# Opening of a two-block transformer kernel: all keys accumulated by groups of two k-tiles as the modulation arrives, with the output gates' projections between the keys' convolutions

## The chip, the core and the metric

The kernel runs on one core of a Trainium2 chip. The metric is the device time of one execution in microseconds. The engines are TensorE (PE, its weight loads PEld), VectorE (DVE), ScalarE (ACT), GpSimd (POOL) and SyncE (SP), which issues the transfers.

## What is computed

A token sequence x (256 tokens, 1024 features) goes through a first block that also reads a context ctx (256 tokens), and then through two layers of feed-forward, mixer, feed-forward. The change lies at the start of the first block. Cut to that:

```
shift, scale, gate       = split(silu(c) @ w_mod + b_mod, 3)
shift_c, scale_c, gate_c = split(silu(c_ctx) @ w_mod + b_mod, 3)
h  = rmsnorm(x, norm_w) * (1 + scale) + shift
hc = rmsnorm(ctx, norm_w) * (1 + scale_c) + shift_c
qkv, beta, decay, kb, vb = split(h @ w_state)      # the same for hc, all but q
za, qb, zb, ga, gb       = split(h @ w_rest)
q, k, v = split(silu(short_conv(qkv)))             # 5 taps, 4 heads of 128
oa = gated_delta_rule(q, k, v, g(decay), sigmoid(beta))   # chunks of 64, both directions
ob = attention(rope(norm(qb)), rope(norm(kb)), vb)
y  = sigmoid(ga) * (ya @ w_proj_a) + sigmoid(gb) * (yb @ w_proj_b)
x  = x + gate * (y @ w_out)
```

All data are f32. The projections run as three products in fp32r: each operand is split into a rounded part and its remainder, and low x high, high x high and high x low are added.

## The kernel before

Activations lie transposed: feature on the partition, 8 k-tiles of 128 features, 256 tokens (T) on the free axis. A weight panel is 128 x 1024 f32 (512 KB). `wload` (L93) brings it into one of seven `raw` buffers through SP's queue, ScalarE rounds it into `wh` (L98), VectorE makes the remainder `wl` (L99), of each of which there are four. `mm3` (L102) runs the 24 products of one output tile of 128 features by 256 tokens, L110 to L112.

The order of each engine's instructions is not written out: a planner works it out when the program is built, from the order of the trace, from priorities (`high_priority(offset)` puts a block ahead by that many places; `prior`, L773, does it for a generator) and from its own estimates of durations. `tc.issue_after(ins)` adds an order only: instructions of the block that run on the engine of `ins` are issued behind it. Each engine then runs its list in order. PSUM has eight banks: `pj` 2, `ms` 2, `ch` 3, `md` 1.

**The opening, `b1_hidden` (L921).** The shift and scale of x and ctx (columns of `w_mod`, 2 x 1024) are made in four groups g of 256 features, which are two k-tiles. `mods(g)` (L947) loads the weights of a group. The shift of groups 0 and 2 is made on VectorE: a panel is multiplied by a row of silu(c) or silu(c_ctx), spread over all partitions by `mod_row` (L726), and summed (L954), eight such instructions. The other six products of 256 columns run on TensorE with two stationary columns (c and c_ctx, tile `cc`) and the raw weights as the moving operand, 8 products each (`psm`, L967), one PSUM tile of two rows; ScalarE copies the rows out (L969) and TensorE transposes them to columns (`m1t`, L972). `stats` (L939) squares and adds the 8 k-tiles of x or ctx, sums them over the partitions (`pss`, L165), takes the power on GpSimd (L170), spreads it (`rb`, L173) and multiplies the tiles (L945). `hidden` (L980) applies scale and shift on ScalarE (L984) and splits into `hH` and `hL`. Order of the trace: mods(0), x, mods(1), ctx, stats of x, stats of ctx, mods(2), hidden(0) of x, mods(3), the rest of hidden. All of `b1_hidden` is traced ahead of the first projection.

**Then, `block1` (L782):** the row for c_2, constants, `b1_bd` (L1038: beta and decay, `w_bd`, 48 products with 16 stationary columns), `gates` (L1119: decays, their sums, the factors E0 and E1 through `gps` and four `gdf` products, all banks from `ch`), `b1_keys` (L1076: for each of four heads `b1_both` (L1029) runs 24 products for x and 24 for ctx into `psk`; five-tap convolution on VectorE, L1009; four transposes `ktp` into a `ch` bank, L1095; squares on ScalarE), the first step of `gdn_inverse` (L1257, products of the keys with each other, times E), the kv projection of the attention (`att_k`, `att_v`), and the values of four heads with a step of the inverse between each. After that follow 32 projections of x alone, `rest` (L817): the output gates gb (8, tanh into `tb`), qb (4), q (4), zb, za, ga, each with steps of the inverse, the attention and the chain of the delta rule (`gdn_chain`) between. The block ends with the merge: `branch("w_b")`, `gdn_out` (L1449, gives `ya`), `branch("w_a")`, and `w_out`.

The heart of the opening's TensorE part:

```
for i, raw in enumerate(raws):                       # L964
    for j in range(4):
        k = 4 * i + j
        nc.tensor.matmul(o, c2[:, k, :], raw[:, j * T : (j + 1) * T], start=k == 0, stop=k == 7)
```

Of the kernel before, what the change touches and what calls it, by code (L numbers as in the profile page):

```python
# [37 lines left out]
class Kern:  # L38
# [63 lines left out]
    def mm3(self, ps, W, h, kw, kh, first, last):  # L102
# [4 lines left out]
        for i, (a, b) in enumerate(zip(kw, kh)):  # L107
# [4 lines left out]
            mm(ps, H[:, s], hL[:, b, :T], start=False, stop=l)  # L112
# [669 lines left out]
    def block1(self):  # L782
        nc, A = self.nc, self.A
        with ExitStack() as c:
# [5 lines left out]
            gates = self.gates()  # L790
            gb = self.b1_bd(hx, hc)
            for _ in self.prior(gates(gb), 600):
                pass
            self.b1_rope_consts()
            self.b1_keys(hx, hc)
            inv = self.prior(self.gdn_inverse(), 1500)
            next(inv)
            ak = self.att_k(self.b1_both(A["w_kv"][0], hx, hc))
            next(ak)
            self.att_v(self.b1_both(A["w_kv"][1], hx, hc))  # L800
            for h in range(4):
                next(inv)
                self.b1_value(h, hx, hc)
            four = lambda n, t: self.yy.tile([P, KD, T + 2], F32, tag=t, name=n)
            pair = lambda n, t: four(n, t)[:, :, :T].rearrange("p (i h) t -> p i h t", i=2)
            Q2 = pair("Q2", "hHc")
            self.qT, self.qr = Q2[:, 0], Q2[:, 1]

            self.MT = four("MT", "hLc").rearrange("p k t -> p (k t)")[:, : 4 * 512].rearrange("p (b n m t) -> p b n m t", b=2, n=2, t=P)
            self.Db = pb.tile([P, 2, 4, P], F32, tag="Ec", name="Db")  # L810
            nc.gpsimd.memset(self.MT, 0.0)
            nc.gpsimd.memset(self.Db, 0.0)
            self.nqa = pb.tile([P, 2, 2, 4], F32, name="anq")
            self.nqg = pb.tile([P, 2, 4], F32, name="gnq")
# [21 lines left out]
            for kind, n in (("gb", 8), ("qb", 4), ("q", 4)):  # L836
                for i in range(n):
                    if kind == "gb" and i == 4:
                        next(ak)
# [81 lines left out]
    def b1_hidden(self):  # L921
# [24 lines left out]

        def mods(g, after=None):  # L947
            a = slice(2 * g, 2 * g + 2)
            fast = g % 2 == 0
            if fast:  # L950
                for k in (2 * g, 2 * g + 1):
                    raw = self.wraw(self.A["wmod_sh"][g + k % 2], 1024)
# [788 lines left out]
```

## Time and profile before

| | us |
|---|---|
| median of 3 runs | 1442.99 |
| lowest, highest run | 1441.73, 1444.32 |
| profiled execution | 1442.31 |
| its span | 1440.5 |
| TensorE busy in it | 1403.3 (97%) |
| VectorE busy | 1141.0 (79%) |
| ScalarE busy | 771.0 (54%) |
| GpSimd busy | 85.7 (6%) |
| mean rate of the transfers | 211 GB/s |

The span is that of one profiled execution; its instructions are laid out by engine, with the idle time before each and what ended it. The execution took 1.8 us more than the span, and 0.7 us less than the median. A product of plain f32 operands leaves two records in the trace, one of fp32r operands or a transpose leaves one. Lengths of products overlap, as they are pipelined: the time from start to start counts.

### The profile page before, as it was taken

The numbers are of one execution on the slowest core, as the hardware profiler recorded it, in microseconds if no ns is written. First come the engines' busy times: TensorE is split into PE (matmuls) and PEld (weight loads), VectorE is DVE, ScalarE is ACT, GpSimd is POOL, SyncE is SP. The second block draws the span as 40 slices with busy tenths as digits, with TensorE's granted clock in tenths as the row PEclk, the third lists the DMA queues.
The fourth block names the chain that finished last, engine by engine and source line by source line (L and its number), as shares of the span: only waits on it lengthen the run. The fifth ranks groups of instructions, "written<-read, shape, count | busy, mean of one in ns | idle before, by whom it ended". The sixth has DMA issues, their size and how long they took to land. (4 is left out here: it accounts for less than half of the span.)

```text
span 1440.5 us, 27393 instructions
## 1 busy us (share of the span) xinstructions
PE 1403.3 (97%) x10786; PEld 1305.3 (91%) x10786; DVE 1141.0 (79%) x2124; ACT 771.0 (54%) x1315; POOL 85.7 (6%) x87
## 2 busy tenths in 40 slices
PE   7999989999999999999999999999999999999998
PEld 4798867889999989998899998999989998899997
DVE  6769888858887887888897797977688889796554
ACT  4654586644644446447564444544446357554442
POOL 0011100012100001001100001000011010100000
PEclk9999999999999999999999999999999999999999
DMA  8524545635688985557568897688774557577562
GB/s 317 195 64 124 150 147 174 222 103 164 198 288 276 323 286 182 176 153 252 171 202 303 271 356 243 201 283 286 237 255 158 172 175 234 175 242 241 172 199 70
DMA packets 94833, 303.98 MB, mean 211 GB/s; under 512 B 18128, under 2 KB 20432, under 8 KB 94448
## 3 DMA queue, kind: packets, MB, share of 16 engines
q1 hardware_dynamic: 89824, 299.90, 63.3%
q8 instruction: 85, 1.39, 0.4%
q10 hardware_dynamic: 4432, 1.11, 0.4%
q0 software_dynamic: 448, 1.21, 0.3%
q14 instruction: 44, 0.36, 0.1%
HBM read 300.09 MB, written 2.10 MB: 210 GB/s over the span
## 5 line engine op out<-in xcount | busy, mean ns | idle before, releaser
L98 ACT CAST wh<-raw 128x1024 fp32r<-128x1024 f32 (+3 forms) x407 | 414.6, 1021 | 288.2 <-PE psd L121 89.1
L99 DVE TENSOR_TENSOR wl<-raw,wh 128x1024 fp32r<-128x1024 f32 (+3 forms) x407 | 481.5, 1187 | 94.5 <-ACT wh L98 93.6
L111 PE MATMUL psf<-hH,wh 128*128 128x256 f32 x1088 | 306.1, 281 | 0.0
L112 PE MATMUL psf<-hL,wh 128*128 128x256 f32 x1088 | 305.6, 281 | 0.0
L110 PE MATMUL psf<-hH,wl 128*128 128x256 f32 x1088 | 305.4, 281 | 0.0
L121 PE MATMUL psd<-gHL,wh 128*128 128x512 f32 x704 | 244.3, 392 | 0.0
L744 DVE CUSTOM_DVE_ANT_0 raw<-raw,mrow 128x1024 f32<-128x1024 f32 x152 | 184.5, 1219 | 69.7 <-DMA raw<-in_wmod 68.1
L110 PEld LDWEIGHTS psf<-hH,wl 128*128 128x128 f32 x1088 | 205.6, 189 | 0.0
L112 PEld LDWEIGHTS psf<-hL,wh 128*128 128x128 f32 x1088 | 205.5, 189 | 0.0
L111 PEld LDWEIGHTS psf<-hH,wh 128*128 128x128 f32 x1088 | 204.8, 188 | 0.0
L122 PE MATMUL psd<-gHL,wl 128*128 128x256 f32 x704 | 196.8, 280 | 0.0
L121 PEld LDWEIGHTS psd<-gHL,wh 128*128 128x128 f32 x704 | 132.2, 188 | 29.0
L110 PE MATMUL psp<-hH,wl 128*128 128x256 f32 x512 | 149.6, 292 | 2.4 <-DVE wl L99 2.4
L111 PE MATMUL psp<-hH,wh 128*128 128x256 f32 x512 | 148.2, 289 | 0.0
L112 PE MATMUL psp<-hL,wh 128*128 128x256 f32 x512 | 147.0, 287 | 0.0
L122 PEld LDWEIGHTS psd<-gHL,wl 128*128 128x128 f32 x704 | 132.2, 188 | 0.0
L110 PEld LDWEIGHTS psp<-hH,wl 128*128 128x128 f32 x512 | 97.7, 191 | 5.5 <-PE psp L112 1.7
L112 PEld LDWEIGHTS psp<-hL,wh 128*128 128x128 f32 x512 | 97.7, 191 | 1.6 <-issue 1.0
L111 PEld LDWEIGHTS psp<-hH,wh 128*128 128x128 f32 x512 | 97.3, 190 | 1.2 <-issue 0.7
L249 ACT ACTIVATE ft<-psf 128x256 f32<-128x256 f32 x68 | 26.2, 386 | 112.2 <-PE psf L112 112.2
L157 POOL TENSOR_TENSOR sqa<-sqa,sq 128x256 f32<-128x256 f32 x36 | 31.3, 868 | 593.9 <-issue 481.3
L252 ACT CAST gHL<-ft 128x256 fp32r<-128x256 f32 x88 | 35.7, 406 | 28.1 <-DVE ft L250 22.3
(513 smaller groups left out, 2789.3 us busy)
## 6 DMA issues: line engine op xcount, KB each, us to landing
raw<-in_ffn_gu SPq DMA_DIRECT2D x176, 512.0 KB, 4.4
raw<-in_wmod SPq DMA_DIRECT2D x144, 512.0 KB, 4.5
raw<-in_ffn_dn SPq DMA_DIRECT2D x64, 448.0 KB, 4.1
raw<-in_win SPq DMA_DIRECT2D x56, 512.0 KB, 4.3
raw<-in_w_rest SPq DMA_DIRECT2D x32, 512.0 KB, 3.8
raw<-in_ffn_dn SPq DMA_DIRECT2D x32, 512.0 KB, 4.6
raw<-in_wmod_sc SPq DMA_DIRECT2D x12, 512.0 KB, 7.4
raw<-in_wout_a SPq DMA_DIRECT2D x16, 384.0 KB, 4.0
```

The costliest lines, as they stand in the source:

```text
L98: nc.scalar.copy(H[:, :n], raw[:, :n])
L99: nc.vector.tensor_sub(L[:, :n], raw[:, :n], H[:, :n].bitcast(F32))
L110: mm(ps, L[:, s], hH[:, b, :T], start=f, stop=False)
L111: mm(ps, H[:, s], hH[:, b, :T], start=False, stop=False)
L112: mm(ps, H[:, s], hL[:, b, :T], start=False, stop=l)
L121: mm(ps, H[:, s], h[:, b, :, :T], start=first and i == 0, stop=False)
L122: mm(ps[:, 1, :], L[:, s], h[:, b, 0, :T], start=False, stop=last and i == len(kw) - 1)
L157: self.seng.tensor_add(self.sqa, self.sqa, o)
L249: nc.scalar.activation(t, ps[:, 0, :], AF.Silu)
L252: nc.scalar.copy(gH[:, f, :], t)
L744: nc.vector.tensor_tensor_reduce(raw, raw, row, op0=ALU.mult, op1=ALU.add, scale=1.0, scalar=0.0, accum_out=t[:, j : j + 1])
```

## The change

Layout on the host: `w_mod`'s shift and scale columns lie by group (`wmod_s`: for each g, shift then scale, two raws each), and the keys' weights by group too (`w_kg[g]`: k-tiles 2g and 2g+1 of all four heads in one panel).

`b1_hidden` loads x and ctx ahead of the modulation's weights, and `w_bd` next. All sixteen modulation raws go to TensorE. The stationary operand has 32 columns (c, c_ctx and thirty zeros); of the four k-tiles in a raw each writes another 32 partitions of one bank, so four partial sums stand below one another. ScalarE copies the bank (128 x 512), and products with `sel`, a 128 x 2 matrix of ones at partitions 32j and 32j+1, add the four partial sums and turn rows into columns at once. The row of c_ctx and VectorE's reductions are gone. When a group's hidden tiles are there, `products(g)` adds its two k-tiles to all four heads' keys and to `w_bd`, for x and ctx, 60 products a group, into five PSUM banks that are held throughout (`pj`, `md`, `ch`, `ch`, `pj`).

`block1` then runs the kv projections first; the gates are issued behind the first of them, a head's convolution and transposes (priority 400 for 150) behind the projection before, with one projection of gb between heads; the inverse starts behind the fourth. The other four projections of gb follow the values one by one.

```
@@ mm3
+            self.last = mm(ps, H[:, s], hL[:, b, :T], start=False, stop=l)
@@ block1
-            gates = self.gates()
-            gb = self.b1_bd(hx, hc)
-            for _ in self.prior(gates(gb), 600):
-                pass
-            self.b1_rope_consts()
-            self.b1_keys(hx, hc)
-            inv = self.prior(self.gdn_inverse(), 1500)
-            next(inv)
-            ak = self.att_k(self.b1_both(A["w_kv"][0], hx, hc))
-            next(ak)
-            self.att_v(self.b1_both(A["w_kv"][1], hx, hc))
-            for h in range(4):
-                next(inv)
-                self.b1_value(h, hx, hc)
...
+            gates = self.gates()
+            gb = self.b1_bd(hx, hc)
+            ak = self.att_k(self.b1_both(A["w_kv"][0], hx, hc))
+            next(ak)
+            with self.tc.issue_after(self.last.ins):
+                for _ in self.prior(gates(gb), 600):
+                    pass
+            self.b1_rope_consts()
+            self.att_v(self.b1_both(A["w_kv"][1], hx, hc))
+            keys = self.b1_keys()
+            for i in range(4):
+                with self.tc.issue_after(self.last.ins):
+                    next(keys)
+                rest("gb", i)
+            next(keys, None)
+            inv = self.prior(self.gdn_inverse(), 1500)
+            with self.tc.issue_after(self.last.ins):
+                next(inv)
+            for h in range(4):
+                self.b1_value(h, hx, hc)
+                next(inv)
+                rest("gb", 4 + h)
+                if h == 1:
+                    next(ak)
...
-            for kind, n in (("gb", 8), ("qb", 4), ("q", 4)):
+            for kind, n in (("qb", 4), ("q", 4)):
...
@@ b1_hidden
-        c2 = pb.tile([P, KD, 2], F32, tag="gg", name="cc2")
+        c2 = pb.tile([P, KD, 32], F32, tag="E0", name="cc2")
+        nc.vector.memset(c2, 0.0)
...
+        sel = pb.tile([P, 2], F32, tag="gy", name="sel2")
+        nc.vector.reduce_sum(sel, self.ident.rearrange("p (g c) -> p c g", g=4)[:, 0:2, :], axis=AX.X)
...
+        def mods(g):
+            ps = self.chbank("psm1").rearrange("p (k t) -> p k t", t=T)
+            for kind in range(2):
+                for i in range(2):
+                    raw = self.wraw(self.A["wmod_s"][4 * g + 2 * kind + i], 1024)
+                    for j in range(4):
+                        nc.tensor.matmul(ps[32 * j : 32 * j + 32, kind, :], c2[:, 4 * i + j, :], raw[:, j * T : (j + 1) * T],
+                                         start=i == 0, stop=i == 1, skip_group_check=True)
+            row = pb.tile([P, 2, T], F32, tag="tg", name="mrow", bufs=2)
+            nc.scalar.copy(row, ps)
...
+                    nc.tensor.matmul(t[:, n : n + 2], row[:, kind, j * P : (j + 1) * P], sel, start=True, stop=True)
...
+        def products(g):
+            W = Wk[g]
+            for h in range(5):
+                for s in range(2):
+                    for j in range(2):
+                        k = 2 * g + j
+                        (WH, WL), w = (W, slice((2 * h + j) * P, (2 * h + j + 1) * P)) if h < 4 else (W_bd, slice(16 * k, 16 * k + 16))
+                        o = acc[h][:, s, :] if h < 4 else acc[h][0:16, s, :]
+                        hH, hL = (a[:, k, :T] for a in out[s])
+                        for i, (x, y) in enumerate(((WL, hH), (WH, hH), (WH, hL))):
+                            nc.tensor.matmul(o, x[:, w], y, start=k + s + i == 0, stop=k == 7 and i == 2, skip_group_check=True)
...
+        nc.sync.dma_start(self.xT, self.A["x"])
+        nc.sync.dma_start(ctxT, self.A["ctx"])
+        W_bd = self.wload(self.A["w_bd"], P)
+        mods(0)
+        acc = [p.tile([P, 2, T], F32, tag=t, name="psk")
+               for p, t in ((self.pj, "pj"), (self.md, "md"), (self.ch, "ch"), (self.ch, "ch"), (self.pj, "pj"))]
         stats(self.xT, xs)
+        Wk = [self.wload(self.A["w_kg"][0])]
         stats(ctxT, ctxT)
+        hidden(0)
         self.seng = nc.gpsimd
+        for g in range(1, 4):
+            mods(g)
+            Wk.append(self.wload(self.A["w_kg"][g]))
+            products(g - 1)
+            hidden(g)
+        products(3)
+        self.acc = acc
...
@@ b1_bd
-        H, L = self.wload(self.A["w_bd"], P)
...
+        ps = self.acc[4]
@@ b1_keys
-            ps = self.b1_both(A["w_k"][h], hx, hc)
+            ps = self.acc[h]
...
-            with self.tc.high_priority(offset=150):
+            with self.tc.high_priority(offset=400):
...
+            yield
```

## Rows read from the trace of the kernel before

**Rows 1.** Busy time by stretch: length, busy us (instructions) by engine, clock, DMA share, GB/s.
```profile
0.00:49.90 49.90, 40.87 (x228) 24.50 (x229) 31.77 (x112) 29.18 (x70) 3.29 (x9) 1.00 0.84 301
49.90:97.00 47.10, 47.09 (x359) 42.74 (x358) 33.00 (x76) 24.54 (x69) 5.42 (x2) 1.00 0.35 107
97.00:160.00 63.00, 60.37 (x484) 58.92 (x483) 58.87 (x122) 29.91 (x62) 4.58 (x3) 0.97 0.43 126
```

**Rows 2.** Groups by line and shape, 0 to 50 us: busy, mean ns, idle before.
```profile
L967 PE MATMUL psm<-raw,cc 128*2 128x256 f32 x96 | 22.2, 379 | 0.0
...
L734 PE MATMUL mr<-ident,sc_c_ctx 128*128 128x128 f32 x16 | 3.1, 378 | 0.0
...
L972 PE MATMUL m1t<-ident,mrow 2*128 2x2 f32 x12 | 1.7, 207 | 1.6 <-ACT mrow L969 1.6
...
L165 PE MATMUL pss<-ones,sqa 128*128 128x1 f32 x8 | 1.2, 252 | 1.5 <-DVE sqa L157 1.5
...
L954 DVE CUSTOM_DVE_ANT_0 mjk<-raw,mrow 128x1024 f32<-128x1024 f32 x4 | 4.9, 1219 | 1.8 <-ACT mrow L735 1.8
```

**Rows 3.** TensorE's timeline, opening: start, length, instruction, count, idle before.
```profile
4.46 3.79 PE L734 MATMUL mr<-ident,sc_c 128*128 128x128 f32 x16 [4.46 <-DVE sc_c L723]
...
11.08 3.61 PE L967 MATMUL psm<-raw,cc 128*2 128x256 f32 x16
...
20.19 0.60 PE L165 MATMUL pss<-ones,sqa 128*128 128x1 f32 x4
...
49.83 0.28 PE L1050 MATMUL psb<-hL,wh 128*16 128x256 f32 x1
...
49.95 0.28 PE L110 MATMUL psk<-hH,wl 128*128 128x256 f32 x1
```

**Rows 4.** TensorE's timeline, where products use column groups.
```profile
194.12 0.28 PE L111 MATMUL psp<-hH,wh 128*128 128x256 f32 x1
194.33 0.43 PE L1540 MATMUL apv<-aw,vza 128*64 128x128 f32 x2
194.70 0.39 PE L112 MATMUL psp<-hL,wh 128*128 128x256 f32 x1
...
638.35 0.65 PE L361 MATMUL pv<-sw,vz 128*64 128x256 f32 x4
```

**Rows 5.** Stretches chosen by the transfers.
```profile
0.00:2.75 2.75, 0.00 (x0) 0.00 (x0) 0.31 (x7) 1.28 (x1) 1.31 (x6) 1.00 0.40 89
2.75:24.75 22.00, 19.81 (x104) 13.46 (x105) 13.10 (x57) 9.81 (x27) 0.70 (x1) 1.00 1.00 398
```

**Rows 6.** ScalarE's timeline.
```profile
12.25 0.42 ACT L155 ACTIVATE sqa<-xT 128x256 f32<-128x256 f32 x1 [0.48 <-DMA xT<-in_x]
...
67.55 0.60 ACT L1179 ACTIVATE E<-gdf 128x512 f32<-128x512 f32 x1 [0.26 <-PE gdf L1178]
...
70.93 0.37 ACT L1097 COPY ktc<-ktp 128x256 f32<-128x256 f32 x1
```

**Rows 7.** VectorE's timeline.
```profile
23.03 2.48 DVE L945 TENSOR_TENSOR xs<-xT,rb 128x512 f32<-128x512 f32 x4 [1.59 <-DMA raw<-in_wmod_sc]
...
94.56 1.22 DVE L1273 TENSOR_TENSOR E<-E,gc 128x1024 f32<-128x1024 f32 x1
...
331.59 0.42 DVE L290 TENSOR_TENSOR yaL<-gya,yaH 128x256 fp32r<-128x256 f32 x1
```

**Rows 8.** TensorE's timeline, keys' transposes and the last merge.
```profile
67.35 0.27 PE L1095 MATMUL ktp<-ident,kTx 128*128 128x128 f32 x1
...
92.90 0.33 PE L1095 MATMUL ktp<-ident,kTc 128*128 128x128 f32 x1
...
336.08 0.36 PE L110 MATMUL psm<-yaH,wl 128*128 128x256 f32 x1
```

**Rows 9.** VectorE's groups, 49.9 to 97 us.
```profile
L99 DVE TENSOR_TENSOR wl<-raw,wh 128x1024 fp32r<-128x1024 f32 x8 | 9.7, 1220 | 0.0
...
L1009 DVE SCALAR_TENSOR_TENSOR cvk<-psk,cwh,cvk 128x508 f32<-128x508 f32 (+1 forms) x12 | 8.9, 746 | 3.3 <-ACT cvk L1005 3.2
```

More of the change, by code (lines that the diff above doesn't have):

```diff
@@ L945, in stats @@
                 nc.vector.tensor_mul(o[:, k : k + 2, :], x[:, k : k + 2, :], rb[:, None, :T].broadcast_to([P, 2, T]))
[L947 to L952, printed above, removed]
-                    for i in range(2):
-                        nc.vector.tensor_tensor_reduce(raw if i else junk, raw, rows[i], op0=ALU.mult, op1=ALU.add, scale=1.0, scalar=0.0,
-                                                       accum_out=mm[:, 0, k, i : i + 1])
-            t = self.msbank("m1t")
-            for kind in range(int(fast), 2):
-                ps = self.pj.tile([P, 2, T], F32, tag="pj", name="psm1")
-                o = ps[0:2, 0, :]
-                raws = [self.wraw(self.A["wmod_sc"][2 * (2 + g if kind else g // 2) + i], 1024) for i in range(2)]
-                if after:
-                    nc.sync.dma_start(after[0], self.A[after[1]])
-                    after = None
-                for i, raw in enumerate(raws):
-                    for j in range(4):
-                        k = 4 * i + j
-                        nc.tensor.matmul(o, c2[:, k, :], raw[:, j * T : (j + 1) * T], start=k == 0, stop=k == 7)
-                row = pb.tile([P, T], F32, tag="tg", name="mrow", bufs=2)
-                nc.scalar.copy(row[0:2, :], o)
@@ new lines, in mods @@
+        def mods(g):
[8 more added lines that the diff above has]
+            nc.scalar.copy(row, ps)
+            t = self.msbank("m1t")
+            for kind in range(2):
@@ L970, in mods @@
                 for j in range(2):
                     n = 4 * kind + 2 * j
-                    nc.tensor.transpose(t[:, n : n + 2], row[0:2, j * P : (j + 1) * P], self.ident[0:2, 0:2])
-            for kind in range(2):
-                d = mm[:, kind, a, :]
-                src = d if fast and not kind else t[:, 4 * kind : 4 * kind + 4].rearrange("p (a b) -> p a b", b=2)
-                nc.vector.tensor_add(d, src, self.v("b_mod", 8 * kind + 2 * g, 2)[:, :, None].broadcast_to([P, 2, 2]))
+                    nc.tensor.matmul(t[:, n : n + 2], row[:, kind, j * P : (j + 1) * P], sel, start=True, stop=True)
@@ L1043, in b1_bd @@
         gb = pb.tile([P, 2, 4, 8], F32, name="gb")
-        H, L = self.wload(self.A["w_bd"], P)
-        ps = self.pj.tile([P, 2, T], F32, tag="pj", name="psb")
-        for s, h in enumerate((hx, hc)):
-            for k in range(KD):
-                w = slice(16 * k, 16 * k + 16)
-                for i, (a, b) in enumerate(((L, h[0]), (H, h[0]), (H, h[1]))):
-                    nc.tensor.matmul(ps[0:16, s, :], a[:, w], b[:, k, :T], start=k + i == 0, stop=k == 7 and i == 2)
+        ps = self.acc[4]
         y = pb.tile([P, 2, T], F32, tag="ksq", name="gby", bufs=2)
@@ L1674, in layout @@
     w = x["w_mod"][0]
[L1675 to L1676 removed]
+    A["wmod_s"] = np.concatenate([panelV(w[:, (4 * kind + g) * T : (4 * kind + g + 1) * T]) for g in range(4) for kind in range(2)])
     A["wmod_g"] = panelR(w[:, 2048:])
```

53 lines of the change are left out of this document (21 added, 32 removed).

## The prediction

> **What bounds the kernel now.** I read the busy times by stretch first, then TensorE's groups in the opening, then its timeline. The stretches [rows 1] show TensorE busy 40.87 of the first 49.9 us, all of the next 47.1, and 60.37 of the 63 after that: behind the opening TensorE is the bound, and time is won by taking work or waits off it. VectorE is idle for 18.1 us of the opening and 14.1 us of the next stretch, but only for 4.1 of the 63 us from 97 to 160. So there is a second bound close behind: the chain keys, gates, inverse, GDN chain, `gdn_out`, in which VectorE's part is large. The granted clock is 1.00 (the 2.4 GHz level) in both early stretches, so I expect no gain or loss from the clock.
>
> In the opening the modulation products `psm` are 96 records, 22.2 us busy [rows 2]. Sixteen of them take 3.61 us; without the last one's 0.38 that is 0.215 us from one to the next [rows 3]. The first projection record starts at 49.95, 0.12 us behind the last of `w_bd` [rows 3].
>
> **The change part by part, on TensorE.** Measure: when are the 240 products of `w_bd` and the keys done, with nothing but the opening's own work beside them? Before: 49.95 plus 192 key products at 0.12, that is 73.0 us.
> - The context's row `crow` goes: -3.1 us, its 16 records [rows 2].
> - `psm` becomes 64 products (128 records) of 32 stationary columns, four column groups each. One behind the other they cost 128 x 0.215 = 27.5 us, four at a time 6.9. No row shows four, but two: four records of 256 columns in two column groups, `pv`, take 0.65 us in all [rows 4], where four in line would start over 0.645 us and end after 1.0. I take 8.5: fourfold overlap, and 0.1 for each of the 16 raws, which land singly. Against 22.2 that is -13.7.
> - The 12 transposes `m1t` (1.7 us) become 16 products with `sel`, 32 records of one full weight load and two columns. Their nearest row is `pss`: four records in 0.60 us, the last 0.25 of it its own length, so 0.12 from start to start [rows 2, 3]. 3.8 us: +2.1.
> - TensorE's own waits in the opening are 49.9 - 40.87 - 4.46 at the start = 4.6 us [rows 1, 3]. All of them hang on `psm`, row copies and statistics in an order that is gone: -4.6, and new ones are counted below.
>
> That gives 73.0 - 3.1 - 13.7 + 2.1 - 4.6 = 53.7 us if TensorE never waits. The new waits:
> - The transfers. 16 raws, four key panels, x, ctx, `w_bd` and the small ones are some 12.9 MB. At 89 GB/s for 2.75 us and 398 GB/s after that [rows 5] the last lands at 34.5 us. Conversion and the last group's hidden rows and 60 products fit into the 19 us left, so DMA is not the end of this stretch unless the seven raw buffers starve it.
> - The statistics. x is issued ahead of the raws and lands at some 5.2 us by the same rates. From x's first square (12.25) to its last normalised tile (23.03 + 2.48) it is 13.3 us now [rows 6, 7]; so x is ready at 18.5. ctx follows between 21.0 (only its multiplication behind x's) and 31.8 (another 13.3). TensorE has work without ctx up to 53.7, less the 210 later products (25.2) and half of `psm` and `sel` (6.2), that is 22.3 us. The wait lies between 0 and 9.5; I take 3, as squares of ctx can run under x's sums and multiplications.
> - Changes between column groups and whole-array products. Around the two `apv` records the next whole-array record starts 0.21 and 0.37 us on, where 0.12 and some 0.11 would do: 0.35 us more for a return trip [rows 4]. The first group meets no key products; for the other 12 raws that is 0 to 4.2 us, and I take 1.5, since raws may be consumed in pairs.
>
> The Trainium skill, "TensorEngine Tiling (Array Packing)", section Key Properties, says that a change of tiling mode drains TensorE, which speaks against this change. The trace agrees in sign with its 0.35 us; by that rule applied at every raw the term would be 4.2 instead of 1.5 and the sum would be 2.7 us later.
>
> So the 240 products end at 53.7 + 3 + 1.5 = 58.2 instead of 73.0: TensorE's work is **14.8 us ahead**.
>
> On VectorE eight reductions of 1.22 us go, 9.8 us with their reads [rows 2]; the four key panels' remainders (1.22 each) only move earlier, into its idle time. The memset, `sel` and its sum are single small instructions in VectorE's early idle time: nothing, and under 1 us if that cover were gone, as TensorE's first product waits for VectorE already. On SP the moved x and ctx go past up to six raws, and four key panels past `b1_consts`, whose tables are wanted only by the gates. 16 raws before, 16 after: no bytes are saved.
>
> **What of it is kept.** All heads and `w_bd` now end together, so what hung on the early ones starts late. TensorE has cover: two kv projections (96 products) and the output gates between heads, 24 each. `issue_after` only fixes an order; nothing idles for it unless a transpose stands at TensorE's head before VectorE's convolution is done. VectorE has 16 taps of 0.75 us and six remainders of 1.22 [rows 9], with the gates some 30 us of work from head 0's end on, about as long as TensorE's. The inverse starts behind the last head's transposes: before, the last transpose was at 92.90 and the first product with E at 94.56, 1.7 us on [rows 7, 8]. After: 58.2, 96 + 72 products (20.2), and the small products. Those are what 49.9 to 97 holds beside its 288 large ones, 47.1 - 34.6 = 12.5, of which I put 3 behind the last transpose as the inverse's own: 9.5. With 1.7 that is 89.6. The **chain starts 5.0 us earlier**, not 14.8.
>
> At the end of the block the last `yaL` is ready at 331.59 + 0.42, and TensorE reaches its product at 336.08 [rows 7, 8]: 4.1 us of slack. TensorE's lead is therefore worth 5.0 + 4.1 = **9.1 us** when the chain takes as long as before; what lies over that turns into waits between 97 and 336. Later stages see the same instructions: 0.
>
> Sum: the profiled execution took 1442.31 (span 1440.5 and 1.8 around it); 1433.2 after. The median of the runs is 0.7 above that execution, so **1434**.
>
> **Rivals.**
> 1. *The chain shortens too.* It shares TensorE with fill that is now done earlier, and VectorE lost 9.8 us of work. Then all 14.8 us are kept, 1428, and with waits and changes at 0 19.3 us, 1424. For: VectorE's idle time early on [rows 1]. Against: from 97 to 160 VectorE is 93% busy with the same steps. 0.17.
> 2. *The lead stays, the chain doesn't move.* VectorE's 30 us get gaps, or ctx comes at 31.8; the chain starts at 96 to 101, and 1440 to 1446 results. 0.18.
> 3. *Slower: one free `ch` bank.* Heads 2 and 3 hold two of the three banks until their convolutions, so the gates' five uses and the transposes of heads 0 and 1 take turns. E was ready 18.2 us after the last `w_bd` product (49.95 to 67.55 + 0.60) [rows 3, 6]; behind a kv projection (5.8) that is 82.2. A head's transposes hold a bank from 67.35 to 71.30, 3.95 us [rows 6, 8]. Four heads in turn (15.8) and 2.4 for four copies no longer overlapped make 100.4, with the 1.7 102.1: 7.5 late, 4.1 covered, 3.4 us slower, 1447. It decides once the chain starts after 98.7. For: nothing in the chain can be hoisted past a bank. Against: heads 0 and 1 can be transposed before the gates need theirs, and head 2's bank comes free meanwhile. 0.14.
> 4. *The column groups run one behind the other*, so the change doesn't do what it says. `psm` costs 27.5, the 3 us of waits are filled: 74.2, chain at 105.6, 11.0 late, 6.9 us slower, 1450. Against it stands `pv`. 0.06.
>
> **How the numbers follow.** The forecast (1429 to 1439) has 0.45. About 0.2%, 2.9 us, can be told from no change. Faster: 0.45 + 0.17 + 0.03 of rival 2 = 0.65; the rest of rival 2 is within 0.2%, 0.15; rivals 3 and 4 are slower, 0.20. The range reaches from rival 1's best, 1424, to the edge of rival 3, 1446; about 0.2 lie outside.
>
> **What would show it.** Right: four `psm` records starting within some 0.1 us; the last `psk` record of a key near 58; first product with E near 90; TensorE's new idle time between 97 and 200; the last `yaL` close before its product near 327. Wrong: `psm` at 0.215 from record to record; TensorE waiting for raws or ctx beyond 10 us before 58; SP waiting for raw buffers with DMA under 300 GB/s before 33 us; the product with E after 98.7.

## The result, and the profile after

The changed kernel takes 1454.5 us (median of 6 runs, 1450.6 to 1459.4) against 1442.4 before (6 runs beside it, 1440.9 to 1444.3): ratio 1.0085, 95% interval 1.0064 to 1.0106. It is **slower by 12 us**; 1434 with a range of 1424 to 1446 was forecast. The profiled execution took 1453.8 us (span 1452.0). The whole difference arises in block 1: the first product of `w_out` (`pso`) starts at 349.3 us before and at 361.5 after, and what follows takes as long as it did (1090.5 us of the span, before 1091.2).

The stretches of [rows 1], and three more, by the same view of the changed kernel (length, busy us of TensorE, its weight loads, VectorE, ScalarE, GpSimd, granted clock, DMA share, GB/s):
```profile
0.00:49.90 49.90, 38.50 (x288) 28.74 (x292) 24.18 (x90) 24.52 (x56) 3.73 (x9) 1.00 0.80 287
49.90:97.00 47.10, 46.94 (x381) 41.87 (x370) 28.04 (x72) 30.21 (x64) 1.64 (x1) 1.00 0.41 133
97.00:160.00 63.00, 60.26 (x483) 58.91 (x482) 55.05 (x114) 35.07 (x87) 7.48 (x4) 0.97 0.39 116
160.00:200.00 40.00, 27.55 (x164) 23.75 (x163) 32.06 (x86) 21.34 (x50) 5.61 (x2) 0.87 0.45 135
...
20.00:30.00 10.00, 7.36 (x46) 4.21 (x46) 6.23 (x13) 4.01 (x11) 0.65 (x1) 1.00 0.78 271
30.00:40.00 10.00, 9.55 (x86) 8.17 (x86) 5.35 (x12) 5.47 (x12) 0.70 (x1) 1.00 0.47 149
90.00:100.00 10.00, 9.85 (x72) 8.57 (x72) 1.20 (x1) 9.94 (x38) 0.00 (x0) 1.00 0.05 13
```
The kernel before, from 160 to 200 us:
```profile
160.00:200.00 40.00, 34.90 (x264) 29.26 (x264) 32.86 (x85) 31.88 (x76) 4.70 (x2) 1.00 0.49 137
```
TensorE is no busier in the opening (38.50 us, before 40.87 [rows 1]) and has more records done. At 160 to 200 us it is busy for 27.55 of 40 us, where it was for 34.90. At 90 to 100 us VectorE works for 1.20 us and ScalarE for 9.94.

TensorE's timeline in the opening, which answers to [rows 3]:
```profile
12.86 1.08 PE L966 MATMUL psm<-raw,cc 128*32 128x256 f32 x8 [0.20 <-DMA raw<-in_wmod_s]
...
28.24 0.41 PE L999 MATMUL psk<-hH,wl 128*128 128x256 f32 x1
28.45 0.41 PE L999 MATMUL psk<-hH,wh 128*128 128x256 f32 x1
...
49.30 0.28 PE L999 MATMUL psk<-hL,wh 128*16 128x256 f32 x1
49.51 1.93 PE L966 MATMUL psm<-raw,cc 128*32 128x256 f32 x32
51.37 0.38 PE L999 MATMUL psk<-hH,wl 128*128 128x256 f32 x1
51.59 0.28 PE L999 MATMUL psk<-hH,wh 128*128 128x256 f32 x1
...
66.58 0.28 PE L999 MATMUL psk<-hL,wh 128*16 128x256 f32 x1
```
The stretch in which the records run at half the rate of the later ones (columns as above):
```profile
10.00:29.60 19.60, 14.86 (x90) 8.49 (x94) 7.38 (x18) 6.60 (x16) 0.88 (x1) 1.00 0.91 343
```
SP's waits up to 67 us (us in total, times, longest):
```profile
SPq L90 <- PE psm L966: 24.6, 12, 5.6
```
ScalarE's timeline, where the first row's copy stands between the squares of ctx:
```profile
15.28 0.58 ACT L969 COPY mrow<-psm 128x512 f32<-128x512 f32 x1 [4.61 <-PE psm L966]
```
Four column groups do overlap: 32 records of `psm` in 1.93 us. But at 13 us they take twice that (8 in 1.08), and key records start 0.21 us apart at 28, not 0.12. The 1.00 in the clock column is no reading there: the trace of this run holds no record of the granted clock ahead of 29.7 us, and the column counts what isn't recorded as full. The last of the 240 products starts at 66.58 us: 58.2 was forecast. SP stood for 24.6 us before raw buffers that `psm` had not read, but TensorE itself waited for raws for only 2.4 us in all. From 33.1 us to the last of these products it has no wait of note.

The keys' transposes with their squares (all instructions on the tile `ktp`: duration least, median, most; first and last start), for [rows 8]:
```profile
L1111 ACT ACTIVATE ksq<-ktp x16: 268/282/314, 93.6 to 102.3; 128x128 f32<-128x128 f32 x16
L1110 PE MATMUL ktp<-ident,kTx x8: 271/302/328, 90.9 to 99.7; 128*128 128x128 f32 x8
L1110 PE MATMUL ktp<-ident,kTc x8: 271/274/333, 95.2 to 101.6; 128*128 128x128 f32 x8
```
ScalarE's timeline ahead of them, for [rows 6]:
```profile
89.08 0.60 ACT L1195 ACTIVATE E<-gdf 128x512 f32<-128x512 f32 x1 [0.26 <-PE gdf L1194]
89.70 1.28 ACT L1044 ACT_TABLE_LOAD   x1
...
91.32 1.28 ACT L1195 ACT_TABLE_LOAD   x1
92.61 1.09 ACT L1195 ACTIVATE E<-gdf 128x512 f32<-128x512 f32 x2
93.58 0.28 ACT L1111 ACTIVATE ksq<-ktp 128x128 f32<-128x128 f32 x1
```
VectorE's timeline, for [rows 7]:
```profile
98.80 1.23 DVE L99 TENSOR_TENSOR wl<-raw,wh 128x1024 fp32r<-128x1024 f32 x1 [9.02 <-ACT wh L98]
...
105.49 1.22 DVE L1289 TENSOR_TENSOR E<-E,gc 128x1024 f32<-128x1024 f32 x1
...
348.89 0.42 DVE L290 TENSOR_TENSOR yaL<-gya,yaH 128x256 fp32r<-128x256 f32 x1
```
Before, the transposes were spread from 67.35 to 92.90, one head at a time beside the next head's products. Now all 16 squares stand behind the gates' last Exp, and ScalarE needs 93.58 to 102.9 for their squares and copies. Meanwhile VectorE has nothing for 9.02 us. The first product with E, where the inverse starts, comes at 105.49 (before 94.56), the last `yaL` at 348.89 (331.59).

### The profile page after: what moved, and what is told of

Read it like the earlier page. It is cut to its first block, busy times and chain, and to the rows that moved or that the text cites. A ratio compares the mean times of both kernels' runs of the same rounds, so it can differ in the third digit from the quotient of the medians.

```text
span 1452.0 us, 27427 instructions
## 1 busy us (share of the span) xinstructions
PE 1399.9 (96%) x10822; PEld 1306.1 (90%) x10822; DVE 1127.8 (78%) x2106; ACT 769.8 (53%) x1311; POOL 85.0 (6%) x87
## 3 DMA queue, kind: packets, MB, share of 16 engines
q10 hardware_dynamic: 4432, 1.11, 0.3%
## 5 line engine op out<-in xcount | busy, mean ns | idle before, releaser
L99 DVE TENSOR_TENSOR wl<-raw,wh 128x1024 fp32r<-128x1024 f32 (+3 forms) x407 | 481.3, 1186 | 98.3 <-ACT wh L98 97.0
```

The lines of the kernel that those rows point to most:

```text
L99: nc.vector.tensor_sub(L[:, :n], raw[:, :n], H[:, :n].bitcast(F32))
```

## The experiments

Theory A: the loss comes from the order behind the opening, which sends the transposes behind the gates. Theory B: the opening is at fault, since its products end at 66.7 instead of 58.2. Later C: four convolutions, the gates and 16 transposes hang on one moment, when all five accumulators end together. And D: the turn of the `ch` banks. All runs together, each with the kernel before on its chip:

| run | edit of the changed kernel | first product with E, us | first `pso`, us | median, us | ratio to before (95%) |
|---|---|---|---|---|---|
| before | | 94.6 | 349.3 | 1442.4 | |
| after | none | 105.5 | 361.5 | 1454.5 | 1.0085 (1.0064-1.0106) |
| 1 | order of before | 107.7 | 362.0 | 1451.2 | 1.0056 (1.0037-1.0076) |
| 2 | opening of before | 110.1 | 365.3 | 1459.9 | 1.0112 (1.0090-1.0135) |
| 3 | no forced places | 102.8 | 360.5 | 1455.3 | 1.0081 (1.0053-1.0110) |
| 4 | head 3 on Tanh | 107.6 | 365.1 | 1454.4 | 1.0079 (1.0052-1.0106) |
| 5 | statistics first | 104.7 | 363.2 | 1455.1 | 1.0090 (1.0066-1.0113) |
| 6 | `w_bd` first | 103.5 | 359.7 | 1453.7 | 1.0075 (1.0051-1.0098) |
| 7 | gates in `ms` | 106.7 | 361.9 | 1455.2 | 1.0093 (1.0069-1.0116) |
| 8 | 3, 5, 6, 7 and `c_2` early | 105.2 | 361.4 | 1453.9 | 1.0070 (1.0044-1.0097) |
| 9 | 1, 4 to 7 and `c_2` early | 92.9 | 349.9 | 1442.9 | 1.0009 (0.9998-1.0019) |
| 10 | 9, heads 2 and 3 late | 90.6 | 349.1 | 1444.2 | 1.0019 (1.0009-1.0029) |
| 13 | 9 without 4 | 94.2 | 351.7 | 1443.4 | 0.9999 (0.9985-1.0014) |
| 14 | 9 without 1 | 99.5 | 360.2 | 1452.0 | 1.0073 (1.0045-1.0101) |
| 15 | 9 without 7 | 107.8 | 366.2 | 1459.4 | 1.0114 (1.0086-1.0141) |
| 17 | 1 and 7 only | 96.9 | 356.8 | 1447.7 | 1.0036 (1.0021-1.0052) |
| 11 | before, rows as column groups | 102.7 | 357.8 | 1449.9 | 1.0055 (1.0035-1.0075) |
| 12 | 11 and idle products | 105.6 | 358.3 | 1453.6 | 1.0082 (1.0062-1.0103) |
| 16 | 10, four `ga` ahead of `q` | 88.9 | 359.5 | 1452.4 | 1.0067 (1.0046-1.0088) |
| 18 | 10, idle products before `gx` | 90.1 | 357.0 | 1449.1 | 1.0039 (1.0024-1.0054) |

### The two halves (1 to 3)

Run 1, the order of before behind the new opening:
```diff
+for _ in self.prior(gates(gb), 600): pass
+self.b1_rope_consts()
+for _ in self.b1_keys(): pass
+inv = self.prior(self.gdn_inverse(), 1500)
+next(inv)
 ak = self.att_k(self.b1_both(A["w_kv"][0], hx, hc))
...
```


> The new opening (groups of two k-tiles, products in order of arrival) with the order of before behind it: gates, the four keys' convolutions and transposes without the forced places, the inverse's first step, then both kv projections, the four values, the eight gb projections. Theory A (the loss is the new order behind the opening: gates and key transposes queue behind the kv projections, and the inverse starts late): the keys' transposes spread over about 68 to 90 us again, the first product with E stands at 86 to 97 us instead of 105.5, the first step of the inverse (XW) at or before 113 us, the block's end (first pso) at 342 to 351 us instead of 361.5, the time 1433 to 1444 us. Theory B (the opening itself is at fault, its products end at 66.7 us where I had 58.2): the order behind it matters little, first product with E after 102 us, the time 1449 to 1456 us.

Run 2, the opening of before, `w_bd` and the keys over all eight k-tiles into the same five accumulators, then the order of the change.

> The opening of before (shifts and scales of c and c_ctx as before, hidden states whole), then w_bd and the four keys' products over all eight k-tiles into the same five accumulators as the change, and from there the order of the change. Theory A: the late inverse is there without the new opening; the first product with E comes 27 to 37 us behind the last key product (38.8 in the change), the time is 1452 to 1466 us, above the kernel before. Theory B: without the new opening most of the loss is gone, 1440 to 1446 us.

Run 3:
```diff
-with self.tc.issue_after(self.last.ins):
-    for _ in self.prior(gates(gb), 600): pass
+for _ in self.prior(gates(gb), 600): pass
```
and likewise round the keys and the inverse's first step.

> The change without its six issue_after scopes (gates, four keys, first step of the inverse are no longer kept behind the product that was traced last); all else stays, the trace order too. Theory A in its narrow form (the forced places are what sends the key transposes behind the second kv projection, 81.9 us): gates ready 5 to 12 us earlier than 93.7, key transposes start near 70 us, first product with E at 90 to 98 us, the time 1440 to 1447 us. Rival (the order is made by priority and by ScalarE's load, the scopes bind nothing): first product with E stays within 2 us of 105.5, the time 1452 to 1457 us.

Each half alone is slower than before, and the two do not add: 0.56% with the new opening, 1.12% with the new order, 0.85% with both. Run 1 came out as B said, run 2 as A said. So A as I put it fell in run 1 (first product with E at 107.7, not 86 to 97): there the gates are traced ahead of the keys, and all transposes come at 98.4 to 106.0, behind them. B fell in run 2 (1459.9, not 1440 to 1446). No gain or loss by the forced places can be told: without them the time is the same.

The profiled execution of run 1 differs from that of the change in one more thing. Its stretch at 30 to 40 us:
```profile
30.00:40.00 10.00, 10.00 (x49) 8.35 (x48) 4.32 (x9) 3.22 (x6) 0.70 (x1) 0.50 0.30 97
```
Its granted clock is 0.50 until 42.7 us, and the last of the 240 products starts at 72.3. The same opening has its last at 66.6 to 66.8 in the change and in runs 3 and 7, where the half rate ends at about 30, and at 69.9 and 70.1 in runs 4 and 17, where it lasts, with one break, to 40.6. So up to 5.7 us of run 1's late start of E are the clock's; without them it would still be near 102.

### One suspect at a time (4 to 8)

Run 4: `self.conv(cv[:, h % 2], ps, 4 + h, False)`.

> The change with head 3 of the keys on the Tanh path as heads 0 to 2 are, so that no Silu stands between the gates' Exp; all else stays. If the four table loads of 1.28 us at 84 to 93 us, in the saturated ScalarE, are a term of the loss: two to four of them go, the first product with E comes 2.5 to 5 us earlier (100.5 to 103), the time 1449 to 1452 us. If they lie beside another wait: within 1 us of the change, 1453 to 1456 us.

Run 5: `stats(self.xT, xs)` and `stats(ctxT, ctxT)` ahead of `mods(0)`.

> The change with the statistics of x and ctx traced ahead of the first group's shift and scale rows, nothing else: TensorE's pss and rb records come before psm, and ScalarE's squares of ctx are not interrupted by the copy of the first row. Theory B2 (the opening is late because the in-order queues of TensorE and ScalarE held x's and ctx's statistics behind rows that waited for transfers): x normalised at 11 to 17 us instead of 22.0, ctx at 17 to 24 instead of 33.3, key products dense from 24 to 28 us instead of 33, the last one at 58 to 62 us instead of 66.7; the time 1449 to 1453 us if the chain follows by 3 to 6 us. Rival (the transfers through seven raw buffers pace the groups anyway): products end within 2 us of 66.7, the time 1453 to 1456 us.

Run 6, without the forced places too: in the last group `for h in (4, 0, 1, 2, 3)`.

> The change without its issue_after scopes (as the run without forced places) and with the 12 w_bd products ahead of the keys' 48 in the last group, so that gby can be copied some 5.5 us earlier (61 instead of 67 us). Theory C (the arrival order lets all five accumulators end together, w_bd at 66.7 us where it ended at 49.8, and the gates' serial chain that hangs on w_bd sets the start of the inverse): gates ready 3 to 6 us earlier than 93.2, first product with E at 100 to 103, the time 1450 to 1453 us. Rival (VectorE's and ScalarE's queues are full of the keys' convolutions, which come at once): gates ready within 1.5 us of 93.2, the time 1453 to 1457 us.

Run 7, without the forced places too: `self.msbank("gps")` and `self.msbank("gdf")`.

> The change without its issue_after scopes and with the gates' five PSUM tiles (gps, four gdf) in the pool ms instead of ch, so that the keys' transposes (ktp, in ch) no longer take their banks in turn behind the gates'. Theory D (the turn of the ch banks, handed out in traced order, keeps all transposes behind gdf): transposes of heads 0 and 1 start at 72 to 80 us instead of 91, ScalarE's 16 squares are done by 93 to 97 instead of 102, first product with E at 95 to 100 instead of 105, the time 1446 to 1451 us. Rival (transposes wait for ScalarE and for the planner's order, not for banks): first transposes after 86 us, first product with E within 2 us of 105, the time 1453 to 1457 us.

Run 8 is 5, 6 and 7 together, without forced places, and with the row of `c_2` made beside that of `c`.

> Statistics first, w_bd first in the last group, gates' tiles in ms, no issue_after scopes, and in addition the row of c_2 made at the start of the opening instead of behind the products. If the three causes add up: products end 58 to 62, gates ready 75 to 84, first product with E at 84 to 93 (before: 94.6), last yaL at 320 to 334, the time 1430 to 1442 us. If the chain, once started, is slowed by VectorE as in the change (17 us late at the end of XW where it started 11 late): 1440 to 1448 us. If neither banks nor queue order were the cause: 1448 to 1455 us.

None of them gains anything that can be told from the change, not even run 8. Run 5 shows why the opening stays late: ctx's statistics do come earlier, but TensorE is at the 1.2 GHz level at 20 to 30 us, and its first key product is later than in the change (29.27, there 25.72):
```profile
20.00:30.00 10.00, 9.09 (x50) 5.28 (x51) 4.77 (x10) 3.70 (x8) 0.70 (x1) 0.50 0.44 156
```
```profile
29.27 0.58 PE L999 MATMUL psk<-hH,wl 128*128 128x256 f32 x1 [0.17 <-ACT hH L289]
```
From there TensorE has no gap, and from 30.3 the records start 0.12 us apart: 240 products need 28.8 us, the rows still to be made and the changes between them and the keys some 8, and the last product starts at 65.8, not at 58 to 62. In run 7 the first transposes come at 71.7 us as D says, but the first square on ScalarE only at 83.0 and the last transpose at 103.9, so D's times for the squares and for E (95 to 100, measured 106.7) fell.

### Everything mended, and one cause taken out (9, 10, 13 to 15, 17)

Run 9 has the order of before and all edits of 4 to 8. In run 10, besides, `w_bd` has a weight tile of its own, and it and heads 0 and 1 alone are multiplied in order of arrival:
```diff
-        products(3)
+        products(3, (4, 0, 1))
+        for g in range(4): products(g, (2,))
+        for g in range(4): products(g, (3,))
```


> The best I can make of the new opening with all five accumulators ending together: statistics first, w_bd first in the last group, row of c_2 in the opening, gates' tiles in ms, the order of before behind the opening without forced places, and head 3 on the Tanh path, so that ScalarE loads no table between the gates' Exp. Theory C (what counts is that four convolutions, the gates and 16 transposes all hang on one moment, about 30 us of VectorE's and 20 us of ScalarE's work that before lay beside the keys' products): first product with E not before 90 us, at 91 to 98, the time 1440 to 1448 us, no gain on before. Theory A2 (the queues' order alone was at fault): first product with E at 84 to 90, the time 1432 to 1440 us.

> The same with the arrival order for w_bd and heads 0 and 1 alone (36 products a group); heads 2 and 3 follow head by head over all four groups once the hidden states are whole, and w_bd has its own weight tile. Theory C: w_bd and heads 0 and 1 end some 6 to 10 us before the last product, their convolutions and transposes lie beside the products of heads 2 and 3, first product with E 2 to 7 us earlier than in the run with all at once. Theory A2: no difference above 1.5 us, or a loss, if TensorE stands still for transfers in the first groups.

Run 9 has lost the loss: 1442.9 us, ratio 1.0009, with all five accumulators still ending in the last group (`w_bd` at 60.5 us, the keys by 66.2). That is what C had said of this run, no gain on before with E at 91 to 98, and not what A2 had. But the loss is gone while the common end is still there, so C is not what makes the change slower. Run 10, with the ends apart, has E 2.3 us earlier and brings no time. Then I took single parts out of run 9 again:

> The all-at-once run (1442.9 us) with head 3 of the keys back on the Silu path of the change, all else as there. If the table loads of 1.28 us between Silu, the gates' Exp and the squares are a cause that only shows once banks and order are mended: four or more loads appear among 75 and 100 us, first product with E 3 to 9 us later than 92.9, the time 1446 to 1451 us. If they are none (as the run with the Tanh path alone suggests): first product with E within 1.5 us of 92.9, the time 1441 to 1444.5 us.

> The all-at-once run with the traced order of the change behind the opening (kv projection, gates, second kv projection, keys, gb projections between them; no forced places), all else as there, Tanh path and banks too. If the order of the change is the main cause: ScalarE's queue holds head 2 and 3's convolutions behind the kv projection's sum of squares again, first product with E at 98 to 104, the time 1448 to 1454 us. If the banks and the table loads were: first product with E at 91 to 95, the time 1441 to 1445 us.

> The all-at-once run with the gates' five tiles back in the pool ch, traced ahead of the key transposes, all else as there. If the turn of the ch banks is the main cause: all 16 transposes stand behind gdf (first one after 85 us), first product with E at 98 to 104, the time 1448 to 1454 us. If not: transposes from 70 us, first product with E at 91 to 95, the time 1441 to 1445 us.

> The change with two edits and no third: the traced order of before behind the opening (alone 1451.2 us) and the gates' five tiles in ms instead of ch (alone 1455.2 us). If these two together are the cause, and the opening's own queue order (statistics, w_bd first, row of c_2) is not: first transposes before 80 us, first product with E at 92 to 97 instead of 105.5, the time 1442 to 1446 us. If the opening's order is needed as well: first product with E at 98 to 103, the time 1447 to 1452 us.

The transposes in run 9:
```profile
L1105 PE MATMUL ktp<-ident,kTx x8: 271/318/330, 69.9 to 82.0; 128*128 128x128 f32 x8
L1105 PE MATMUL ktp<-ident,kTc x8: 270/319/329, 71.7 to 84.2; 128*128 128x128 f32 x8
```
The same in run 15, which differs in the pool of five tiles alone:
```profile
L1105 PE MATMUL ktp<-ident,kTx x8: 272/286/327, 98.3 to 104.4; 128*128 128x128 f32 x8
L1105 PE MATMUL ktp<-ident,kTc x8: 272/323/329, 100.7 to 106.1; 128*128 128x128 f32 x8
```
With the gates in `ch` the first transpose comes at 98.3 us instead of 69.9, behind the last `gdf`, and the kernel is 15 us slower than run 9 by the two ratios: **the banks alone are enough for the loss**. With the change's order (run 14) it is 9 us slower by the ratios, and ScalarE's timeline shows what stands in its queue:
```profile
73.02 0.60 ACT L415 ACTIVATE sq<-psk 128x512 f32<-128x512 f32 x1 [2.47 <-PE psk L112]
73.51 0.68 ACT L1023 ACTIVATE cvk<-psk,cwh 128x512 f32<-128x512 f32 x1
```
VectorE's timeline in the same run:
```profile
74.76 0.17 DVE L431 TENSOR_SCALAR aka<-nka 128x8 f32<-128x8 f32 x1 [1.73 <-PE nka L418]
...
82.91 0.74 DVE L1027 SCALAR_TENSOR_TENSOR cvk<-psk,cwh,cvk 128x508 f32<-128x508 f32 x1
```
VectorE's timeline in run 9:
```profile
72.23 5.33 DVE L1025 SCALAR_TENSOR_TENSOR cvk<-psk,cwh,cvk 128x508 f32<-128x508 f32 x8 [0.17 <-ACT cvk L1021]
```
ScalarE waits 2.47 us for the kv projection's product, with head 2's convolution behind it, and VectorE 1.73 us for that projection's norms, with the gates behind it. The eight taps of heads 2 and 3, in one piece in run 9 and done at 77.6 us, stand between the gates' steps in run 14, the last done at 83.7; the last transpose starts at 97.8 instead of 84.2. How the 13.6 us divide among these was not tested. **The order is the other cause, and it too is enough alone**: hence nothing clear of the noise was gained when only one of them was mended (runs 1 and 7). The Silu path is no cause (run 13). The two alone mend 7 of the 12 us (run 17); statistics, `w_bd` first and the row of `c_2` together the other 5 by the ratios (13 against 17), though none of them showed a gain without the two (runs 5, 6 and 8). Which of the three it is was not tested.

### The shift and scale rows alone (11, 12)

Run 11 is the kernel before with `mods` and `hidden` of the change and the statistics first, and nothing else of it; run 12 adds behind each panel
```diff
+for j in range(3):
+    nc.tensor.matmul(t[:, P : 2 * P], self.ident, self.ident, start=True, stop=True)
```


> The kernel before with one part of the change alone: shifts and scales of all four groups as fourfold column groups on TensorE (no row of c_ctx, no reduction on VectorE), statistics traced first, then w_bd and the keys head by head over all k-tiles, and the order of before for all that follows. Theory C: the part that saves TensorE's time is kept and the staggered ends of the keys' products too; w_bd ends at 40 to 45 us instead of 49.8, first product with E at 85 to 91 instead of 94.6, the time 1434 to 1440 us. Rival (the opening is paced by the transfers of 16 panels and its saving is hidden): w_bd ends at 48 to 51, the time 1441 to 1445 us.

> The run before this with three idle products of the identity by itself behind each panel's products (48 in all, into a spare part of the m1t bank), so that TensorE does not stand still while panels arrive. If the granted clock of the opening falls because TensorE stands still (records of 0.21 us start to start instead of 0.118 at 25 to 29 us in the change): the records of w_bd and of the first key head run at 0.11 to 0.12 us from the first on, w_bd ends 1 to 4 us earlier than in the run without them. If the pauses are not what sets the clock: no difference, or up to 2 us later by the added records.

My expectation of run 11 fell: `w_bd` ends at 58.2 us instead of 49.8, and the time is 1449.9. TensorE's timeline there:
```profile
44.09 1.07 PE L957 MATMUL psm<-raw,cc 128*32 128x256 f32 x16
45.87 1.05 PE L965 MATMUL m1t<-sel,mrow 128*128 128x2 f32 x8 [0.70 <-ACT mrow L960]
51.39 0.40 PE L1039 MATMUL psb<-hH,wl 128*16 128x256 f32 x1 [4.47 <-DVE wl L99]
```
Two stretches of run 11 (columns as above):
```profile
20.00:30.00 10.00, 9.40 (x59) 5.72 (x59) 4.27 (x11) 4.23 (x10) 0.70 (x1) 0.50 0.59 200
30.00:40.00 10.00, 9.13 (x58) 6.00 (x59) 2.31 (x9) 5.29 (x14) 0.40 (x1) 0.50 0.86 288
```
The same two stretches in run 12:
```profile
20.00:30.00 10.00, 9.97 (x84) 7.78 (x83) 3.73 (x9) 3.32 (x8) 0.70 (x1) 0.83 0.49 150
30.00:40.00 10.00, 10.00 (x96) 6.72 (x88) 2.62 (x8) 5.01 (x12) 0.00 (x0) 1.00 0.86 282
```
TensorE's timeline in run 12, idle products and the start of `w_bd`:
```profile
30.20 0.94 PE L961 MATMUL m1t<-ident 128*128 128x128 f32 x6
...
53.60 0.40 PE L1041 MATMUL psb<-hH,wl 128*16 128x256 f32 x1 [4.46 <-DVE wl L99]
53.80 0.42 PE L1041 MATMUL psb<-hH,wh 128*16 128x256 f32 x1
```
The last panel is multiplied at 44 to 45 us though it was issued at 33.4. Before, VectorE read four of the 16 panels as they landed; now all pass through TensorE's one queue, between statistics and rows. Then TensorE waits 4.47 us for the remainder of `w_bd`, whose copy stands in ScalarE's queue behind the last group's hidden rows. Idle products keep the clock up while they last (0.83 and 1.00 instead of 0.50), and yet `w_bd` ends 2.9 us later. That does not clear the half rate: the 96 added records take TensorE's time too, six of them 0.94 us, and after the last panel TensorE waits 4.46 us here as well, and the records of `w_bd` start 0.21 us apart again, where I had expected 0.11 to 0.12. What the half rate costs in this stretch stays open; the 4.5 us wait is there at either clock.

### Where the lead goes (16, 18)

In run 10 the chain starts at 90.6, a microsecond from the 89.6 of the forecast, and there is no gain. The same marks of the chain in four traces, in us (`Db` are solved blocks copied for TensorE, `gx` and `gy` the products that join them to the inverse, `gp` the chain's first product with its state):

| | before | after | run 9 | run 10 |
|---|---|---|---|---|
| first product with E | 94.6 | 105.5 | 92.9 | 90.6 |
| last step on XW, the inverse's solved blocks | 162.8 | 180.5 | 168.5 | 162.2 |
| first `gx` from `Db` | 173.4 | 193.6 | 179.5 | 174.9 |
| first `gp` | 197.4 | 216.8 | 204.0 | 205.2 |
| first `pso` | 349.3 | 361.5 | 349.9 | 349.1 |

From E to XW the chain takes 68 us before, 75 in the change, 76 in run 9 and 72 in run 10. Behind `gp` up to 8 us are made up again. TensorE's timeline in run 10:
```profile
174.88 2.05 PE L1363 MATMUL gx<-Db,MT 128*128 128x128 f32 x8 [6.51 <-DVE Db L1357]
177.60 2.08 PE L1369 MATMUL gy<-MT,gxs 128*128 128x128 f32 x8 [0.68 <-ACT gxs L1365]
...
191.66 1.11 PE L1363 MATMUL gx<-Db,MT 128*128 128x128 f32 x8
```
Two stretches of run 10:
```profile
170.00:180.00 10.00, 4.45 (x19) 4.19 (x20) 8.39 (x26) 8.98 (x28) 0.00 (x0) 0.64 0.72 160
180.00:190.00 10.00, 9.33 (x58) 8.50 (x59) 7.02 (x19) 7.80 (x23) 0.00 (x0) 0.68 0.15 43
```
XW is solved at 162.2 us (before 162.8), so that 0.6 of the 4 us is left there, and the first `gp` starts at 205.2 (before 197.4), where run 10 is 7.8 late; the first `pso` is level again. TensorE has nothing to do for 6.51 us before `Db`, and then runs `gx` and `gy` in 2.05 and 2.08 us, a later `gx` in 1.11. From there to `gp` run 10 takes 30.3 us, runs 16 and 18, whose first `gx` is as slow, 32.6 and 31.7; before, the change and run 9, whose first `gx` takes 1.13 us, 23.2 to 24.5. That speaks for the clock, but it compares traces and tests nothing.

Run 16: `for j in range(4): rest("ga", j)` ahead of the `q` projections.

> The run with two heads late (chain start 90.6 instead of 94.6, yet no gain: first product of the chain with the state, gp, at 205.2 instead of 197.4, TensorE busy 4.45 of 10 us at 170 to 180 and at half clock in 170 to 190) with four of the eight ga projections traced ahead of the q projections, so that TensorE has products that wait for nothing while the inverse is solved. If the lead is given back because TensorE runs out of work there, falls to the lower clock and then does the inverse's own products slowly (gx 2.05 instead of 1.13 us): gx at 1.1 to 1.3 us, granted clock above 0.9 in 170 to 200, gp at 195 to 202, the time 1436 to 1441 us. If VectorE and ScalarE set that stretch: gp within 2 us of 205, the time 1442 to 1446 us.

Run 18:
```diff
+if s == 1 and i == 0:
+    for m in range(20):
+        mm(x[:, 0:P], self.ident, W1[:, 0:P], start=True, stop=True)
```


> The run with two heads late (1444.15 us) with 20 idle products of the identity by the solved XW, into the bank that gx overwrites, so that TensorE has 5.4 us more to do between the end of XW (162 us) and Db (174.9 us), where it stood still for 6.5 us and then ran gx in 2.05 and gy in 2.08 us at a granted clock of 0.64 to 0.68. If the standstill is what lowers the clock and the clock is what gives the lead back: gx and gy at 1.1 to 1.3 us, clock above 0.85 in 170 to 190, gp at 199 to 203 instead of 205.2, the time 1438 to 1443 us. If the clock costs nothing there, since the copies between gx and gy set the pace: gp within 1.5 us of 205, the time 1443 to 1446 us.

Both missed. In run 16 my edit could not work: `ta` takes the buffer that the inverse's `Mc` holds, so its first copy comes at 189.7 us; TensorE stood still for 7.28 us before `gx` all the same, and the `q` projections came later. In run 18 the planned order moved with the added products, and a standstill of 4.31 us stayed, as TensorE's timeline of run 18 shows:
```profile
162.40 4.73 PE L1364 MATMUL gx<-XW,ident 128*128 128x128 f32 x40
175.61 2.04 PE L1366 MATMUL gx<-Db,MT 128*128 128x128 f32 x8 [4.31 <-DVE Db L1357]
```
So that TensorE stands still there, and that the products behind are slow, is shown; that this is what gives the lead back is not. Run 9 loses its lead of 1.7 us elsewhere, before XW is solved.

## Why the prediction was wrong

- **`psm` at 8.5 us.** Right at the full clock: 32 records in 1.93 make 7.7 for 128. Rival 4 is out. The return trips were sized well: 0.21 us into the 32 records and 0.22 behind the first whole-array record, where 0.12 would do. The Trainium skill, "TensorEngine Tiling (Array Packing)", section Key Properties, has TensorE drained at a change of tiling mode; the trace shows some 0.2 us a trip for 8 to 32 records at once, and with five trips among the key records some 1.0 us, nearer to my 1.5 than to the 4.2 that I had put on a trip at every raw.
- **58.2 us for the 240 products.** Wrong by 8.5. Two terms failed. The waits: with "All of them hang on `psm` ...: -4.6" and "+3" for ctx, 3 us were put where TensorE waits 6.8 (11.4 idle of 49.9, less 4.6 at the start). ctx is normalised at 35.8, outside the 21.0 to 31.8 that I allowed: its squares waited 4.6 us on ScalarE behind the copy of a row, then for x's sums, then for VectorE, which was multiplying x and making a key panel's remainder. And the clock, "I expect no gain or loss": the records of 10 to 29.6 us run at half rate. Of the 14.86 us that TensorE is busy there half, 7.4, would do at the full one, if no wait took its place; that is an estimate from these rows. "DMA is not the end of this stretch unless the seven raw buffers starve it" is not shown to be wrong: SP waited for them, TensorE hardly did. In no run with the whole new opening did the last product start before 65.8 (72.3 at the latest), so the lead is 7 us at most, not 14.8.
- **"The chain starts 5.0 us earlier."** Wrong, and this is the step that made the sign: 105.5 instead of 89.6. I let TensorE's products set the start. The transposes stood behind the gates' five tiles in `ch`, and then all on ScalarE at once. Rival 3 had this bank, with 0.14, and its sign; I had written against it that heads 0 and 1 can be transposed before the gates need theirs, but banks are handed out in traced order, as run 15 shows. Its start (102.1) came near by luck: it had the gates at 82.2 instead of 93.7, and 18.2 us of turns behind them, where the squares and copies end 9.2 us behind them (102.9).
- **"5.0 + 4.1 = 9.1 us"**, "when the chain takes as long as before". Wrong by itself: with the start at 90.6 (run 10) the time is 1.0019 of that before. The chain takes longer, 3 to 7 us more from E to XW. The slack is there and larger than 4.1: the change is 19.4 us late at `gp` and 12.2 at `pso`. But it was used up by what is lost between E, where the change is 10.9 late, and `gp`.
- Right: nothing changes behind block 1, and "TensorE's new idle time between 97 and 200": from 160 to 200 us TensorE stands for 12.5 us in the change, 9.6 in run 10, and 5.1 before.

Open stay: why run 14, which starts E 6.6 us behind run 9, is 10.3 behind it at `pso`; why the chain takes longer from E to XW; and what gives run 10's lead back. No version was faster than the kernel before.

## What to carry to other kernels

When products are regrouped so that several results end together, list what hangs on each, by engine: work that lay beside the products now lies behind them, and a pool of banks handed out in traced order puts one consumer behind another that used to be early. A lead on one engine turned into standstill here, at the place where the chain is slow; whether work that waits for nothing would keep it, two runs tried and did not show. One mended cause showed nothing here; only taking one out of the fully mended kernel did.

## What the runs showed of the hardware that I had not expected

TensorE in the opening of run 11 ran at a granted clock of 0.50, the 1.2 GHz level, over 20 us in which it was busy 9.40 and 9.13 of 10 us, with 6.22 in the 10 us ahead of them; with idle products between panels it was 0.83 and 1.00. The same opening was granted full clock from about 30 us on in three profiles (the change, runs 3 and 7) and only from 40.6 or 42.7 on, but for one break, in three (runs 4, 17 and 1), and its last product moved with it, from 66.6 to 72.3 us. In the change's own profile the clock column says 1.00 at 20 to 30 us while key records start 0.21 us apart instead of 0.12; the trace holds no record of the clock there, so the records tell the level. Four table loads of 1.28 us each, at 84 to 93 us in a ScalarE that was busy for 9.94 of 10 us, cost nothing that could be measured (run 4 without them, run 13 with two).
